# The first expert gather reads unsplit fp32 tokens for four experts, and the hi/lo split moves behind it

## The chip, the cores and the metric

One core of a Trainium2 chip runs a two-layer decoder trunk on 256 tokens of width 1024. The metric is the device time of one execution in microseconds. Numbers are fp32; where the kernel needs accuracy on TensorE at full rate, an operand is split into two fp32r parts (`h`, the rounded value, and `l`, what is left).

## The reference, cut to what matters

```python
def moe(x, router_w, router_b, w_gate, w_up, w_down):
    aff = sigmoid(xt @ router_w); sel_score = aff + router_b
    # best of 4 groups by its two best scores, then the two best experts in it
    ...
    wts = top_aff / sum(top_aff)
    for e in range(N_EXPERTS):                      # 16 experts of width 512
        he = silu(xt @ w_gate[e]) * (xt @ w_up[e])
        y = y + combine[:, e:e + 1] * (he @ w_down[e])

def reference(x, ...):
    for l in range(DEPTH):                          # 2 layers
        y = mixer(x, ...)                           # three attention branches, gated
        x = layer_norm(DN_ALPHA * x + y, ln1_g[l], ln1_b[l])
        y = moe(x, ...)
        x = layer_norm(DN_ALPHA * x + y, ln2_g[l], ln2_b[l])
```

## The kernel before

Each layer is a mixer and then `moe`. In `moe` the 256 tokens (two tiles `t` of 128) are normalised with the statistics `sc` (mean, `rstd`) that the mixer leaves, `aff` and `sel` give the router's scores, and `msk` marks each token's two experts. Each expert has room for 32 tokens of either tile. A count on TensorE (`pm<-msk,cst`) gives each chosen token its place, `onehot` writes it as ones into `Sx`, and `gather` multiplies the tokens with `Sx`: the result `xe` (feature by expert and place) has the 1024 features as 8 blocks `k`. Before the change the tokens for it are split into `x1h` and `x1l`, stored by blocks `k`, and gathered for 8 experts at a time: `gather(0)` in two halves of four `k` (ahead of the first weight products, and behind the first half of `g` of pair 0), `gather(1)` behind `u` of pair 3. The gather results pass through ScalarE and VectorE, which apply the layer norm's gain and shift.

The experts go by pairs `p` = 0 to 7: `g` (gate), `he` by tanh, `u` (up), and one pair later `turn` (transposition of `he`) and `d` (down). Each of `g`, `u`, `d` of a pair is four loads of 1 MiB, named `w_{g|u|d}_{q}_{a}` in the traces (`q` half of the contraction, `a` expert of the pair). They are issued in one fixed order (g0 u0 g1 u1 d0 g2 u2 d1 ...) on SyncE's queue, which is in order: a load whose slot is not yet free holds back all behind it. Slots are 1 MiB tiles of one pool of 25, `big`, taken in turn as they were released; `x1h`, `x1l`, `xe`, `yt`, `acc` come from it too, `target["o"]` reserves slots for these, and `pump` issues as many loads as `held` permits.

At pair 1, `slot_maps(0)` transposes `Sx` into `st` and sums the combine weights (`cs`), and `accumulator(0)` starts the sum `acc` with the token, times ALPHA, times the norm's gain row (`ps`, made by `ln_rows` from `gcol`). VectorE forms it; GpSimd first adds `x1h` and `x1l` up again.

`warm(n)` issues n transposes on TensorE whose results nobody reads. In the traces all engine instructions stand under line 163 (a helper that records them) and all loads under 221, so names of tiles tell them apart. L1196 is the branch of `over`, which treats tokens that did not fit.

## Time and profile before

| | us |
|---|---|
| median of 3 runs | 843.89 (843.61 to 846.78) |
| the profiled execution | 846.54 |
| its span | 844.7 |
| mean granted TensorE clock in it | 0.993 |
| TensorE busy | 815.4 |

The profiled execution is one of the longer ones; times within it are counted from the span's start. The expert stage of the first layer lies at about 203 to 418 us, that of the second at about 620 to 833.

### The profile page before, as it was taken

Reading aid. Unit: us, or ns where it says so; the run is one execution under the profiler, and the core shown is the slowest. Engines: PE = TensorE matmul, PEld = TensorE weight load, DVE = VectorE, ACT = ScalarE, POOL = GpSimd, SP = SyncE. Lnnn points to the kernel's source line nnn. Section 1 sums busy time; section 2 is a strip of 40 time slices with the busy share of each in tenths; the row PEclk is TensorE's granted clock in tenths of the full one; section 3 lists DMA queues with packets and bytes.
Section 4 is the critical chain, followed back from the end, with each engine's and each line's share of the span. In section 5 each row is a group of like instructions: output and inputs, shape, how many; then the busy total and the mean of one; then the engine's idle time right before and its main releaser. Section 6 shows DMA issues by size and latency. Waiting matters only on the chain.

```text
span 844.7 us, 11443 instructions
## 1 busy us (share of the span) xinstructions
PE 815.4 (97%) x4413; PEld 507.3 (60%) x4413; DVE 432.5 (51%) x898; ACT 289.8 (34%) x507; POOL 98.0 (12%) x90
## 2 busy tenths in 40 slices
PE   7999999999999999997999999999999999999986
PEld 7888778889543443333488877788884434333333
DVE  5798565785332232223388976548761412322244
ACT  5445667344111221110355466654331112111112
POOL 0222221002030000000131232110030300000001
PEclk9999999999999999999999999999999999999998
DMA  9993336995599999999898424478948999999992
GB/s 314 336 385 132 123 127 205 393 350 199 216 421 419 419 419 419 419 419 419 323 386 298 163 77 151 150 258 345 357 177 313 419 420 419 419 419 420 418 411 84
DMA packets 65115, 265.24 MB, mean 314 GB/s; under 512 B 6880, under 2 KB 11168, under 8 KB 40992
## 3 DMA queue, kind: packets, MB, share of 16 engines
q1 hardware_dynamic: 64912, 264.39, 80.3%
q8 instruction: 36, 0.59, 0.3%
q14 instruction: 23, 0.19, 0.1%
q10 hardware_dynamic: 144, 0.07, 0.0%
HBM read 263.39 MB, written 1.05 MB: 313 GB/s over the span
## 4 chain that ended last, share of the span: by engine, by line
PE 42%; DMA 7%; DVE 3%; ACT 0%; POOL 0%; issue 0%; POOLq 0%; ACTq 0%; SPq 0%
PE pm L163 36%; DMA w_d<-in_moe_w_down_dram 5%; PE pt L163 3%; PE ps L163 3%; DMA w_u<-in_moe_w_up_dram 2%; DVE bm L163 1%; DVE acc L163 1%; DVE hl L163 0%; POOLq L1406 0%; POOL acc L163 0%; DVE sel L163 0%; ACT hl L163 0%; DVE mv L163 0%; DVE x1l L163 0%; ACT acc L163 0%
## 5 line engine op out<-in xcount | busy, mean ns | idle before, releaser
L163 PE MATMUL pm<-hl,xh 128*128 128x512 f32 (+2 forms) x704 | 227.2, 390 | 1.5 <-ACT hl L163 1.3
L163 PEld LDWEIGHTS pm<-hl,xh 128*128 128x128 f32 x704 | 131.9, 190 | 29.1 <-issue 4.2
L163 DVE TENSOR_TENSOR hl<-w_in,hl 128x1024 fp32r<-128x1024 f32 (+2 forms) x86 | 104.7, 1228 | 60.6 <-ACT hl L163 57.9
L163 PE MATMUL pm<-hl,xl 128*128 128x512 f32 (+2 forms) x352 | 134.0, 381 | 0.3 <-DVE xl L163 0.3
L163 PE MATMUL pm<-w_d,he 128*64 128x512 f32 x512 | 121.0, 604 | 4.2 <-DVEq L1196 2.8
L163 PE MATMUL pm<-w_g,xe 128*64 128x512 f32 x512 | 115.3, 594 | 3.4 <-DVEq L1196 1.7
L163 PE MATMUL pm<-w_u,xe 128*64 128x512 f32 x512 | 114.9, 593 | 1.5 <-DMA w_u<-in_moe_w_up_dram 1.5
L163 ACT CAST hl<-w_in 128x1024 fp32r<-128x1024 f32 (+2 forms) x88 | 85.7, 1001 | 5.7 <-DMA w_in<-in_w_in_dram 4.9
L163 PEld LDWEIGHTS pm<-w_g,xe 128*64 128x64 f32 x512 | 36.9, 137 | 76.6 <-issue 71.8
L163 PEld LDWEIGHTS pm<-w_u,xe 128*64 128x64 f32 x512 | 38.7, 137 | 73.3 <-issue 67.6
L163 PEld LDWEIGHTS pm<-w_d,he 128*64 128x64 f32 x512 | 37.3, 138 | 74.0 <-issue 67.8
L163 PEld LDWEIGHTS pm<-hl,xl 128*128 128x128 f32 x352 | 67.1, 191 | 10.1 <-DVE xl L163 0.5
L163 DVE SCALAR_TENSOR_TENSOR he<-he,pm 128x512 f32<-128x512 f32 x16 | 17.0, 1063 | 87.8 <-ACT he L163 78.9
L163 DVE TENSOR_TENSOR he<-he,pm 128x512 f32<-128x512 f32 x16 | 17.1, 1069 | 67.1 <-PE pm L163 67.1
L163 PE MATMUL pm<-hl,mh 128*128 128x256 f32 (+1 forms) x192 | 46.5, 325 | 0.0
L163 ACT COPY he<-pm 128x512 f32<-128x512 f32 x14 | 8.2, 587 | 109.7 <-PE pm L163 109.7
L163 ACT ACTIVATE he<-pm 128x512 f32<-128x512 f32 x16 | 17.3, 1080 | 80.8 <-PE pm L163 80.8
L163 DVE SCALAR_TENSOR_TENSOR yt<-pm,cs,yt 128x512 fp32r<-128x512 f32 x32 | 22.9, 747 | 43.0 <-ACT yt L163 42.1
L163 ACT ACTIVATE yt<-pm,cs 128x512 fp32r<-128x512 f32 x32 | 20.8, 686 | 67.4 <-PE pm L163 63.2
L163 POOL TENSOR_TENSOR un<-un,su 128x512 f32<-128x512 f32 x24 | 30.7, 1284 | 95.2 <-DVE su L163 56.9
L163 PE MATMUL pm<-hl,oh 128*128 128x512 f32 x128 | 41.3, 394 | 0.0
L163 POOL TENSOR_TENSOR rstd<-rs,cst 128x1 f32<-128x1 f32 (+1 forms) x6 | 4.2, 692 | 309.5 <-DVE rs L163 309.5
(198 smaller groups left out, 1039.6 us busy)
## 6 DMA issues: line engine op xcount, KB each, us to landing
w_g<-in_moe_w_gate_dram SPq DMA_DIRECT2D x64, 1024.0 KB, 13.6
w_u<-in_moe_w_up_dram SPq DMA_DIRECT2D x64, 1024.0 KB, 14.3
w_d<-in_moe_w_down_dram SPq DMA_DIRECT2D x60, 1024.0 KB, 19.0
w_in<-in_w_in_dram SPq DMA_DIRECT2D x36, 1024.0 KB, 13.4
w_br<-in_w_branch_dram SPq DMA_DIRECT2D x8, 1024.0 KB, 5.1
w_wo<-in_w_o_dram SPq DMA_DIRECT2D x8, 1024.0 KB, 5.0
w_d<-in_moe_w_down_dram SPq DMA_DIRECT2D x8, 512.0 KB, 17.1
w_in<-in_w_in_dram SPq DMA_DIRECT2D x4, 768.0 KB, 8.0
```

The costliest lines, as they stand in the source:

```text
L163: r = f(*args, **kw)
```

## The change

- The normalised token is written once, unsplit, in fp32, by ScalarE into `zk`, laid out by the blocks `k`. `gather(0)` takes only experts 0 to 3, by fp32 products of `zk` with `Sx`. Three rounds of gathering take the place of two: 4, 4 and 8 experts.
- Behind the second half of `gather(0)`, `onehot` for experts 4 to 7 and the split of `zk` into `x1h` and `x1l` (`apart1`) follow; `gather(1)` with them comes behind `g` of pair 1, `gather(2)` where `gather(1)` was.
- `accumulator(0)` reads `zk` (strided) instead of GpSimd's sum, and `zk` is given back there.
- At pair 1 `turn(0)` comes ahead of `slot_maps(0)`.
- The mixer's last stage goes tile by tile instead of by halves of the row; fillers fall from 38 to 32; the reserved slots change.

```diff
-WARM = [38, 6, 12]
+WARM = [32, 6, 12]
...
                 piece(0, 0)
+                piece(1, 0)
+                stat(0, 0)
+                logits(0, 1, 0, halves[0])
                 piece(0, 1)
-                stat(0, 0)
-                piece(1, 0)
-                stat(0, 1)
-                logits(0, 1, 0, halves[0])
-                piece(1, 1)
-                logits(1, 1, 0, halves[0])
-                logits(0, 1, 0, halves[1])
                 stat(1, 0)
                 sc = ln_scales(st[:1])
+                logits(0, 1, 0, halves[1])
+                piece(1, 1)
                 logits(0, 1, 1, halves[0])
+                logits(0, 1, 1, halves[1])
+                stat(0, 1)
+                logits(1, 1, 0, halves[0])
...
     def moe(l, sc, lg, rsum):
-        target["o"] = 5
+        target["o"] = 2
         pump()
-        xh = slot([128, T, KD, 128], F32R, "x1h")
-        xl = slot([128, T, KD, 128], F32R, "x1l")
         warm(WARM[0])
-        xv, hv, lv = xt[0].rearrange("p t (q k) -> p t q k", k=KD), xh.rearrange("p t k q -> p t q k"), \
-            xl.rearrange("p t k q -> p t q k")
+        zk = slot([128, T, KD, 128], F32, "zk")
+        xv, zv = xt[0].rearrange("p t (q k) -> p t q k", k=KD), zk.rearrange("p t k q -> p t q k")
         halves = [slice(0, 512), slice(512, 1024)]
-        def normed(t, k):
-            z = xv[:, t, :, k:k + 4]
-            if t == 0:
-                V.tensor_scalar(z, z, sc[0][0], sc[0][1], op0=OP.subtract, op1=OP.mult)
-            else:
-                A.activation(z, z, AF.Identity, bias=sh, scale=sc[1][1])
-        def high(t, k):
-            A.copy(hv[:, t, :, k:k + 4], xv[:, t, :, k:k + 4])
-        def low(E, t, k):
-            E.tensor_tensor(lv[:, t, :, k:k + 4], xv[:, t, :, k:k + 4], hv[:, t, :, k:k + 4].bitcast(F32), op=OP.subtract)
         aff, sel = small(32, "aff"), small(64, "sel")
         z = [aff[:, NE * t:NE * t + NE] for t in range(T)]
-        normed(0, 0)
-        high(0, 0)
-        low(G, 0, 0)
+        def normed(t, k):
+            A.activation(zv[:, t, :, k:k + 4], xv[:, t, :, k:k + 4], AF.Identity, bias=shs[t], scale=sc[t][1])
+        shs = [ln_shift(*z, name=f"sh{t}") for t, z in enumerate(sc)]
         for t in range(T):
             V.scalar_tensor_tensor(z[t], rsum[:, 0:NE], sc[t][0], lg[t][:, 0:NE], op0=OP.mult, op1=OP.subtract)
+        normed(0, 0)
         for t in range(T):
             V.scalar_tensor_tensor(z[t], z[t], sc[t][1], rsum[:, NE:2 * NE], op0=OP.mult, op1=OP.subtract)
         A.activation(aff, aff, AF.Exp)
-        sh = ln_shift(*sc[1])
         normed(1, 0)
         normed(0, 4)
-        high(0, 4)
-        high(1, 0)
         normed(1, 4)
-        high(1, 4)
-        low(G, 0, 4)
+        drop()
+        xt[0] = None
...
-        low(V, 1, 0)
         comb = small(32, "comb")
         ssum = small(2, "ssum")
         c3 = comb.rearrange("p (t e) -> p t e", t=T)
         warm(WARM[1])
         Sx = {}
-        def onehot(r):
-            Sx[r] = work((128, 8, T, CAP), F32R, name="Sx")
+        def onehot(r, es=range(8)):
+            if r not in Sx:
+                Sx[r] = work((128, 8, T, CAP), F32R, name="Sx")
             for t in range(T):
-                z = (pos if r else pc)[:, NE * t + 8 * r:NE * t + 8 * r + 8, None].to_broadcast([128, 8, CAP])
-                V.tensor_tensor(Sx[r][:, :, t], cc("iota")[:, None, :].to_broadcast([128, 8, CAP]), z, op=OP.is_equal)
-        onehot(0)
+                c = NE * t + 8 * r + es[0]
+                z = (pos if (r, es[0]) != (0, 0) else pc)[:, c:c + len(es), None].to_broadcast([128, len(es), CAP])
+                V.tensor_tensor(Sx[r][:, es[0]:es[-1] + 1, t], cc("iota")[:, None, :].to_broadcast([128, len(es), CAP]), z,
+                                op=OP.is_equal)
+        onehot(0, range(4))
         pos = small(32, "pos")
-        low(G, 1, 4)
         V.tensor_tensor(comb, aff, msk, op=OP.mult)
-        drop()
-        xt[0] = None
         target["o"] = 4
-        pump()
+        ROUNDS = [(0, 4), (4, 4), (8, 8)]
         xe = {}
+        x1 = {}
         def gather(r, ks=range(KD)):
+            e0, n = ROUNDS[r]
             if r not in xe:
-                z = [slot([128, 4, 8, T, CAP], F32, "xe") for i in range(2)]
-                xe[r] = [z[k // 4][:, k % 4] for k in range(KD)]
+                z = [slot([128, 32 // n, n, T, CAP], F32, "xe") for i in range(n // 4)]
+                xe[r] = [z[k * n // 32][:, k % (32 // n)] for k in range(KD)]
             for k in ks:
                 o = (ptp if k % 2 == 0 else psc)()
-                ov_ = o.rearrange("p (e t s) -> p e t s", t=T, e=8)
+                ov_ = o[:, :n * T * CAP].rearrange("p (e t s) -> p e t s", t=T, e=n)
                 for t in range(T):
-                    PE.matmul(ov_[:, :, t], xh[:, t, k], Sx[r][:, :, t], start=True, stop=False)
-                    PE.matmul(ov_[:, :, t], xl[:, t, k], Sx[r][:, :, t], start=False, stop=True)
+                    m = Sx[e0 // 8][:, e0 % 8:e0 % 8 + n, t]
+                    if r == 0:
+                        PE.matmul(ov_[:, :, t], zk[:, t, k], m.bitcast(F32), start=True, stop=True)
+                    else:
+                        PE.matmul(ov_[:, :, t], x1[0][:, t, k], m, start=True, stop=False)
+                        PE.matmul(ov_[:, :, t], x1[1][:, t, k], m, start=False, stop=True)
                 g, b = (gpk[:, l, z, k:k + 1] for z in range(2))
                 if k % 2 == 0:
                     A.activation(xe[r][k], ov_, AF.Identity, bias=b, scale=g)
                 else:
                     V.tensor_scalar(xe[r][k], ov_, g, b, op0=OP.mult, op1=OP.add)
+        def apart1():
+            for i, nm in enumerate(("x1h", "x1l")):
+                x1[i] = slot([128, T, KD, 128], F32R, nm)
+            for t in range(T):
+                split(x1[0][:, t], x1[1][:, t], zk[:, t])
...
-                for t in range(T):
-                    h, lo_ = (z[:, t].rearrange("p k q -> p q k").bitcast(F32) for z in (xh, xl))
-                    G.tensor_tensor(xt[0][:, t].rearrange("p (q k) -> p q k", k=KD), h, lo_, op=OP.add)
             for h in range(2):
                 r = ln_rows(z, l, h, psc)
                 for t in range(T):
                     a = xt[0][:, t, halves[h]]
                     if z == 0:
-                        V.scalar_tensor_tensor(a, a, ALPHA, r, op0=OP.mult, op1=OP.mult)
+                        a, b, c = (y.rearrange("p (q k) -> p q k", k=KD) if y is not None else zv[:, t, 64 * h:64 * h + 64]
+                                   for y in (a, None, r))
+                        V.scalar_tensor_tensor(a, b, ALPHA, c, op0=OP.mult, op1=OP.mult)
...
                 if (nm, p, q) == ("g", 0, 0):
                     gather(0, range(4, KD))
+                    onehot(0, range(4, 8))
+                    apart1()
...
             if p == 1:
+                gather(1)
+                turn(0)
...
                 accumulator(0)
+                drop()
...
-            if p % 4 == 3:
-                drop(2)
+            if p in (1, 3, 7):
+                drop(1 + p // 4)
             if p == 3:
-                gather(1)
+                gather(2)
```

The three places below are of VectorE, TensorE and SyncE.

VectorE in the second layer's router chain, from the maximum over the groups to the one-hot matrix: before,

```order
L163 TENSOR_REDUCE gmax<-pr 128x2
L163 MATCH_REPLACE gr<-gmax,gsum 128x8 x2
L163 SCALAR_TENSOR_TENSOR best<-gr,sel 128x32
L163 MAX mx_5366<-best 128x8 x2
L163 MATCH_REPLACE msk<-mx_5366,best 128x16 x2
L163 TENSOR_SCALAR msk<-msk 128x32
L163 TENSOR_TENSOR x1l<-acc,x1h 128x128x4
L163 TENSOR_TENSOR Sx<-cst,pm 128x8x32 x2
L163 TENSOR_TENSOR comb<-aff,msk 128x32
```

and now:

```order
L163 TENSOR_REDUCE gmax<-pr 128x2
L163 MATCH_REPLACE gr<-gmax,gsum 128x8 x2
L163 SCALAR_TENSOR_TENSOR best<-gr,sel 128x32
L163 MAX mx_5386<-best 128x8 x2
L163 MATCH_REPLACE msk<-mx_5386,best 128x16 x2
L163 TENSOR_SCALAR msk<-msk 128x32
L163 TENSOR_TENSOR Sx<-cst,pm 128x4x32 x2
L163 TENSOR_TENSOR comb<-aff,msk 128x32
L163 TENSOR_SCALAR xe<-ps,gpk 128x256 x2
```

The difference `x1l` between the mask and `Sx` is gone, and `Sx` is made for 4 experts (128x4x32) instead of 8.

TensorE in the first layer, from the end of `g` of pair 1 (`w_g` products) to the first product of `u` (`w_u`): before,

```order
L163 MATMUL pm<-w_g_1_0_1694,xe 64x512
L163 MATMUL pm<-w_g_1_1_1714,xe 64x512
L163 MATMUL pt<-cst,Sx 128x128 x4
L163 MATMUL pt<-comb,Sx 128x32 x4
L163 MATMUL pm<-cst,he 128x128 x4
L163 MATMUL ps<-cst,gcol 128x128 x8
L163 MATMUL pm<-w_u_0_0_1716,xe 64x512
```

and now (the last four of the 32 products of `gather(1)` stand ahead):

```order
L163 MATMUL ps<-Sx,x1h 128x4x32
L163 MATMUL ps<-Sx,x1l 128x4x32
L163 MATMUL ps<-Sx,x1h 128x4x32
L163 MATMUL ps<-Sx,x1l 128x4x32
L163 MATMUL pm<-cst,he 128x128 x4
L163 MATMUL pt<-cst,Sx 128x128 x4
L163 MATMUL pt<-comb,Sx 128x32 x4
L163 MATMUL ps<-cst,gcol 128x128 x8
L163 MATMUL pm<-w_u_0_0_1716,xe 64x512
```

The gather's second round has come in behind `g`, and the turn of `he` (`pm<-cst,he`) stands ahead of the transposes of `Sx` and of the sums with `comb`.

SyncE in the first layer, the last of the loads of `u` of pair 2, the four of `d` of pair 1, and the first two of `g` of pair 3, with the semaphores that each waits for (DMAHW is a DMA lane; the number behind a tile's name is a running one): before,

```order
L221 DMA w_u_1_1_2192<-in_moe_w_up_dram 128x2048 [waits DMAHW3_49,PE_49]
L221 DMA w_d_0_0_2194<-in_moe_w_down_dram 128x2048 [waits DMAHW4_49,PE_49]
L221 DMA w_d_0_1_2215<-in_moe_w_down_dram 128x2048 [waits DMAHW5_49,PE_49]
L221 DMA w_d_1_0_2217<-in_moe_w_down_dram 128x2048 [waits DMAHW6_49,PE_49]
L221 DMA w_d_1_1_2270<-in_moe_w_down_dram 128x2048 [waits DMAHW7_49,PE_49]
L221 DMA w_g_0_0_2272<-in_moe_w_gate_dram 128x2048 [waits DMAHW0_49,PE_49]
L221 DMA w_g_0_1_2282<-in_moe_w_gate_dram 128x2048 [waits DMAHW1_49,PE_49]
```

and now:

```order
L221 DMA w_u_1_1_2181<-in_moe_w_up_dram 128x2048 [waits DMAHW3_49,PE_49]
L221 DMA w_d_0_0_2183<-in_moe_w_down_dram 128x2048 [waits DMAHW4_49,PE_49]
L221 DMA w_d_0_1_2193<-in_moe_w_down_dram 128x2048 [waits DMAHW5_49,PE_49]
L221 DMA w_d_1_0_2195<-in_moe_w_down_dram 128x2048 [waits DMAHW6_49,PE_49]
L221 DMA w_d_1_1_2295<-in_moe_w_down_dram 128x2048 [waits DMAHW7_49,DVE_49,Activation_49]
L221 DMA w_g_0_0_2297<-in_moe_w_gate_dram 128x2048 [waits DMAHW0_49,PE_49]
L221 DMA w_g_0_1_2307<-in_moe_w_gate_dram 128x2048 [waits DMAHW1_49,PE_49]
```

The load `w_d_1_1` waited for TensorE and now waits for VectorE and ScalarE: the slot that it takes was that of a gate weight of pair 1 and is now that of `zk`. The second layer's rows have the same change.

## Rows read from the trace of the kernel before

**Rows 1.** Part 1 of the page: busy time of the engine, share of the span and instructions.

```profile
PE 815.4 (97%) x4413; PEld 507.3 (60%) x4413; DVE 432.5 (51%) x898; ACT 289.8 (34%) x507; POOL 98.0 (12%) x90
```

**Rows 2.** The windows view: for each stretch its length, then busy us and instructions of each engine, the granted TensorE clock, the DMA share and GB/s.

```profile
212.00:216.00 4.00, 3.98 (x18) 3.59 (x20) 2.17 (x4) 1.55 (x2) 0.96 (x1) 0.59 0.49 145
228.00:400.00 172.00, 166.78 (x862) 63.95 (x860) 50.22 (x77) 23.37 (x32) 7.53 (x2) 1.00 1.01 420
399.60:403.00 3.40, 3.40 (x11) 1.20 (x9) 0.00 (x0) 0.00 (x0) 0.00 (x0) 0.50 1.01 410
760.00:820.00 60.00, 57.45 (x294) 21.75 (x290) 19.82 (x27) 9.14 (x13) 0.00 (x0) 1.00 1.01 418
```

**Rows 3.** The chain that ended last, from 755 to 830 us: start us, us, what.

```profile
781.41 19.89 DMA w_u<-in_moe_w_up_dram
...
801.37 19.92 DMA w_d<-in_moe_w_down_dram
```

**Rows 4.** The timeline of TensorE at the end of the first layer's experts: start us, us, engine, line, operation, out<-in, shapes, count, and in brackets the idle time before it and its releaser.

```profile
376.03 3.65 PE L163 MATMUL pm<-w_g,xe 128*64 128x512 f32 x16 [0.35 <-DMA w_g<-in_moe_w_gate_dram]
381.02 3.65 PE L163 MATMUL pm<-w_g,xe 128*64 128x512 f32 x14 [1.34 <-DMA w_g<-in_moe_w_gate_dram]
...
391.00 3.65 PE L163 MATMUL pm<-w_u,xe 128*64 128x512 f32 x14 [0.76 <-DMA w_u<-in_moe_w_up_dram]
...
398.56 5.35 PE L163 MATMUL pm<-w_d,he 128*64 128x512 f32 x16 [2.77 <-DVEq L1196]
```

**Rows 5.** The waits of TensorE from 610 to 835 us: engine, line, what was waited for, us in total, times, longest.

```profile
PE pm L163 <- DMA w_d<-in_moe_w_down_dram: 1.3, 1, 1.3
PE pm L163 <- DMA w_u<-in_moe_w_up_dram: 0.8, 1, 0.8
```

**Rows 6.** The timeline of TensorE, columns as in rows 4, around the first half of the gather: in the first layer (three rows) and in the second.

```profile
210.63 0.41 PE L163 MATMUL pm<-msk,cst 128*128 128x32 f32 x2 [1.60 <-DVE msk L163]
...
212.02 0.55 PE L163 MATMUL pt<-Sx,x1h 128*128 128x256 f32 x1 [0.29 <-DVE Sx L163]
...
215.53 0.65 PE L163 MATMUL pm<-w_g,xe 128*64 128x512 f32 x2
...
628.75 0.36 PE L163 MATMUL pt<-Sx,x1h 128*128 128x256 f32 x1 [0.28 <-DVE Sx L163]
...
630.92 3.65 PE L163 MATMUL pm<-w_g,xe 128*64 128x512 f32 x16
```

**Rows 7.** The timeline of all engines, columns as in rows 4, along the router's chain of the second layer.

```profile
621.24 0.55 DVE L163 TENSOR_SCALAR acc<-acc,mv,rstd 128x512 f32<-128x512 f32 x1
...
621.39 0.80 POOL L163 TENSOR_TENSOR rstd<-rs,cst 128x1 f32<-128x1 f32 x1 [0.26 <-DVE rs L163]
621.43 4.34 PE L163 MATMUL pt<-cst 128*128 128x128 f32 x38
...
623.07 3.34 POOL L163 TENSOR_TENSOR x1l<-acc,x1h 128x512 fp32r<-128x512 f32 x2 [0.88 <-ACT aff L163]
...
623.66 1.09 DVE L163 TENSOR_TENSOR sel<-aff,rb 128x64 f32<-128x64 f32 x1
624.78 0.23 DVE L163 TENSOR_TENSOR pr<-sel 128x64 f32<-128x64 f32 x1
...
625.82 0.64 DVE L163 SCALAR_TENSOR_TENSOR best<-gr,sel 128x32 f32<-128x32 f32 x1
...
627.23 1.06 DVE L163 TENSOR_TENSOR x1l<-acc,x1h 128x512 fp32r<-128x512 f32 x1
...
627.37 0.41 PE L163 MATMUL pm<-msk,cst 128*128 128x32 f32 x2 [1.60 <-DVE msk L163]
...
627.62 0.85 PE L163 MATMUL pt<-cst 128*128 128x128 f32 x6
628.19 0.75 DVE L163 TENSOR_TENSOR Sx<-cst,pm 128x256 fp32r<-128x256 f32 x2
```

**Rows 8.** The same view where pair 1's `g` ends and its `he` and the accumulator are formed (second layer).

```profile
646.98 7.04 PE L163 MATMUL pm<-w_g,xe 128*64 128x512 f32 x32
...
654.15 7.54 POOL L163 TENSOR_TENSOR acc<-x1h,x1l 128x1024 f32<-128x1024 f32 x2 [24.45 <-PE pm L163]
...
656.41 1.10 ACT L163 ACTIVATE he<-pm 128x512 f32<-128x512 f32 x1
...
656.70 7.09 PE L163 MATMUL pm<-w_u,xe 128*64 128x512 f32 x32
...
657.55 1.07 DVE L163 SCALAR_TENSOR_TENSOR he<-he,pm 128x512 f32<-128x512 f32 x1 [1.42 <-ACT he L163]
...
658.53 0.68 DVE L163 SCALAR_TENSOR_TENSOR acc<-acc,ps 128x512 f32<-128x512 f32 x1
...
661.72 1.88 DVE L163 SCALAR_TENSOR_TENSOR acc<-acc,ps 128x512 f32<-128x512 f32 x3 [2.51 <-POOL acc L163]
```

**Rows 9.** The view of one tile on SyncE's queue: first the issue (duration in ns, first and last start), then the time from issue to landing; a `w_g` load issued at 619.2 us into an empty queue, and the last down weight of pair 1 (`w_d_1_1`) at 654.1.

```profile
L221 SPq DMA_DIRECT2D w_g<-in_moe_w_gate_dram x1: 327/327/327, 619.2 to 619.2; - x1
...
DMA to landing us min/median/max: 5.0/5.0/5.0
...
L221 SPq DMA_DIRECT2D w_d<-in_moe_w_down_dram x1: 328/328/328, 654.1 to 654.1; - x1
...
DMA to landing us min/median/max: 12.2/12.2/12.2
```

More of the change, by code (lines that the diff above doesn't have):

```diff
@@ L397, in ln_rows, with ln_shift @@
         return p
-    def ln_shift(mean, rstd):
-        sh = small(1, "sh")
+    def ln_shift(mean, rstd, name="sh"):
+        sh = small(1, name)
         V.scalar_tensor_tensor(sh, mean, -1.0, rstd, op0=OP.mult, op1=OP.mult)
@@ L855, in mixer @@
                 piece(0, 0)
+                piece(1, 0)
+                stat(0, 0)
+                logits(0, 1, 0, halves[0])
                 piece(0, 1)
-                stat(0, 0)
-                piece(1, 0)
-                stat(0, 1)
-                logits(0, 1, 0, halves[0])
-                piece(1, 1)
-                logits(1, 1, 0, halves[0])
-                logits(0, 1, 0, halves[1])
                 stat(1, 0)
                 sc = ln_scales(st[:1])
+                logits(0, 1, 0, halves[1])
+                piece(1, 1)
                 logits(0, 1, 1, halves[0])
+                logits(0, 1, 1, halves[1])
+                stat(0, 1)
+                logits(1, 1, 0, halves[0])
+                stat(1, 1)
+                sc += ln_scales(st[1:])
                 logits(1, 1, 0, halves[1])
                 logits(1, 1, 1, halves[0])
-                logits(0, 1, 1, halves[1])
                 logits(1, 1, 1, halves[1])
-                stat(1, 1)
-                sc += ln_scales(st[1:])
                 drop(3)
@@ L1179, in product @@
             def product(k, a, w):
-                x_ = xe[p // 4][k][:, 2 * (p % 4) + a].rearrange("p t s -> p (t s)")
+                r = min(p // 2, 2)
+                x_ = xe[r][k][:, 2 * p + a - ROUNDS[r][0]].rearrange("p t s -> p (t s)")
                 PE.matmul(o[64 * a:64 * a + 64], x_, w, start=(k == 0), stop=(k == KD - 1))
@@ L1211, in over @@
                     for k in range(KD):
-                        for j, z in enumerate((xh, xl)):
+                        for j, z in enumerate((x1[0], x1[1])):
                             for t in range(T):
@@ L1314, in moe @@
                 tc.mark_branch_hint_location(f"over{l}", engines=[mybir.EngineType.PE])
-            if p == 1:
+            if p == 2:
                 target["o"] = 6
-            if p == 2:
-                target["o"] = 7
             if p == 3:
@@ L1328, in moe @@
             up_("g", p, pg)
+            if p == 0:
+                target["o"] = 6
             if p == 1:
+                gather(1)
+                turn(0)
                 slot_maps(0)
-                turn(0)
             he = hts[p] = work(name="he")
```

## The prediction, on record before the run

> **What bounds the kernel now.** I read the page first: TensorE is busy 97% of the span [rows 1]. The windows view adds the other half: from 228 to 400 us (experts of the first layer) and from 760 to 820 (of the second) the DMA share is 1.01 at about 420 GB/s, while TensorE is busy 166.78 us of 172 and 57.45 of 60 [rows 2]. Which of the two sets the end is told by the chain of waits: its last pieces but the closing ones are two 19.9 us runs of `w_d` and `w_u` loads, not matmuls [rows 3]. A pair of experts is 12 loads of 1 MiB, 30 us at 420 GB/s, and its matmuls take less, so the loads held when the stage starts are eaten up and the last pairs wait for their weights: 0.35 + 1.34 + 0.76 = 2.45 us in the first layer [rows 4] and 0.8 + 1.3 = 2.1 in the second [rows 5]. So each expert stage ends when the weight stream ends. An edit there counts by two things: when the stream begins, and whether it is ever interrupted. TensorE's own work has only these 2.45 and 2.1 us of room before it is the bound.
>
> The profiled execution took 846.54 us, 2.65 over the median of 843.89. Two stretches at half clock make that up. The granted clock is 0.59 from 212 to 216 and 0.50 from 399.6 to 403 [rows 2]. From its first product to the first of `w_g`, the first half of the first layer's gather took 215.53 - 212.02 = 3.51 us, the same work in the second layer 630.92 - 628.75 = 2.17 [rows 6]: 1.34 lost. The sixteen `w_d` products at 398.56 took 5.35 against 3.65 for sixteen others [rows 4]: 1.70 lost. 846.54 - 3.04 = 843.5. Both stretches come behind idle time of TensorE, 1.60 us [rows 6] and 2.77 [rows 4]; but the 1.60 us of the second layer [rows 7] were followed by none. I sum differences on the second layer's rows, which have no such stretch, and set them against the median.
>
> **The change, part by part.** All times are of the second layer before; the first layer does the same.
>
> *Router chain.* `normed` on VectorE, the first rounded copies and GpSimd's differences `x1l` go. `sel` (128x64) took 1.09 us and ended with GpSimd's first difference; `pr` of the same size right behind took 0.23. `best` took 0.64 and ended with GpSimd's second, where the larger `pr` took 0.23 [rows 7]. Without GpSimd I take 0.85 and 0.4 off. Two one-column `sh` steps come ahead, but the 0.55 us `normed` goes, and GpSimd's second `rstd`, 0.80 beside it, may get shorter [rows 7]: together between 0 and -0.3. The mask comes 1.25 to 1.55 us earlier. Behind it VectorE's `x1l` of 1.06 goes and `Sx` is halved; but TensorE's count and its 6 filler products still run 1.1 us from the mask (627.37 to 628.47 [rows 7]), so the gather, which began 1.38 behind it, at 628.75 [rows 6], wins only 0.25 more. The first gather itself costs as before: half the experts, but an fp32 product is issued in two parts, so 16 issues again ahead of the first `w_g` product. That one comes **1.7 us** earlier; bounds 1.3 (no `rstd` gain, `best` barely shorter) and 1.9. The first layer's half-clock stretch may go too (-1.34 on a disturbed execution, nothing on the median): the idle time ahead of the mask's product shrinks from 1.6 to about 1.0, since the mask comes 1.25 earlier and the fillers fall from 38 to 32, 0.7 us at 4.34 / 38 = 0.114 each [rows 7].
>
> *Mixer's last stage.* The same pieces in another order; the last `rs` comes out where it was, as the last piece still ends the product stream. 0, bounds -0.4 and +0.4.
>
> *Second gather.* 32 products of 128 columns are added behind `g` of pair 1, on TensorE, in the path of everything there. None of this form is in the trace. Below: 32 x 0.068 = 2.2 us, if one takes half of a 256-column product (2.17 / 16 = 0.136 [rows 6]). Above: the 128-column fillers, 0.114 each [rows 7], so 3.65 us. These are the nearest in columns, and hardly faster than 256 columns: I take **3.65**. TensorE ends each layer's stage 3.65 - 1.7 = 1.95 later, less than its waits of 2.45 and 2.1, so by itself this is hidden.
>
> *Conversions.* The `x1` copies and differences go to pair 0, where VectorE and ScalarE have room (29 to 33% and 14 to 15% busy over the stage [rows 2]): 0. GpSimd's sum for `acc`, 7.54 us, goes; VectorE waited 2.51 for it [rows 8], and behind it stood only the second step of pair 1's `he`, which needs `u`, ready at 663.8, anyway: 0.
>
> *The load queue.* This decides. Three loads go to slots that are free at the mixer's end, earlier than before, but into a queue idle anyway: 0. One goes later, the last of pair 1's down weights, `w_d_1_1` (the last fences of the change): SyncE's queue is in order, and this load now waits for VectorE's last read of `zk`, the fourth `acc` of pair 1, where it waited for the end of `g`. Before: issued at 654.1, right behind the last `w_g` product (646.98 + 7.04 [rows 8]), it landed 12.2 later, at 666.3, because others were ahead of it; a load issued into an empty queue landed in 5.0 [rows 9]. The stream is thus 7.2 us ahead at this point, and a hold up to that length is free.
>
> Now, without the 1.7: `g` ends at 654.0, the gather at 657.6. Turn, maps and `gcol` rows run there as before, to the first `w_u` at 656.70 + 3.65 = 660.35 [rows 8]. On ScalarE the copy of `he`, the cast of `st` and then tanh (1.10) come in order behind the turn; tanh, which ended at 657.5, ends 2.8 later, at 660.3 (less than 3.65 since the turn now stands ahead of the maps). VectorE's `he` follows, 1.07, to 661.4; then four `acc`. They took 0.68 and 1.88 / 3 = 0.63 [rows 8] on contiguous rows. Now one input is `zk`, read at steps of 512 bytes. `he`, the same operation at the same step, took 1.07 [rows 8]; bounds 0.63 and 1.07, and I take 1.0, being nearest in kind to `he`. The last ends at 665.4, the load is issued at 665.5 and lands at 670.5: 4.2 later than before. The hold is 11.4, the cover 7.2. The eight loads ahead run dry, and everything behind is late by 4.2 - 1.7 = **2.5 us per layer**, 5.0 in both; TensorE's own shift of 1.95 lies inside it. With contiguous prices: 663.9, 2.7 - 1.7 = 1.0 per layer.
>
> The Trainium skill has a rule that speaks to this price (SBUF — State Buffer, in the section Door 1: The DMA port swizzle, its note on cachelines): consecutive accesses within one 16-byte line run at full bandwidth, each access to a new line pays a penalty. By that rule the `acc` with `zk` is slower than the contiguous one and the sum is the 5.0, without it the 2.0; the rows of `he` and `acc`, 1.07 against 0.63 to 0.68, agree, but for a strided output, not a strided input.
>
> **Sum.** 2 x 2.5 = +5.0 on 843.9: **848.9 us** (851.5 for an execution with both half-clock stretches).
>
> **Rivals.**
> - *Hold covered, TensorE the bound.* If the last `acc` ends before 661.2, as it would if tanh and `he` were done during the second gather, or the loads ahead took longer, the stream is not interrupted. It would then win 1.7, but TensorE's 1.95 uses up the waits: 1.95 - 2.45 = -0.5 and 1.95 - 2.1 = -0.15. Together -0.65: 843.2. For it: tanh needs only `g`. Against: on ScalarE it stands behind the turn's copy, in program order. 0.17.
> - *Short hold.* The strided input costs nothing and the 128-column products half: hold shorter by 1.5 + 1.45, 2.5 - 2.95 = -0.45 per layer: 843.0. One of the two alone gives +2.0 or +2.1, 845.9 to 846.0. For it: the output is contiguous. Against: the row of the fillers. 0.25 for either or both.
> - *More than the hold.* The empty queue makes later loads late too, or TensorE, idle longer before its last `w_d`, falls to half clock where it hadn't (1.34 to 1.7 each): +6.5 to +9, 850.5 to 853. For it: such stretches follow waits of 1.6 to 2.8 us in this trace, and the waits grow. 0.13.
> - *All gains, no cost.* Cheap products and a covered hold: -1.7 on each stream and TensorE far enough ahead, with the mixer's order winning 0.4 per layer: -4.2, 839.7. 0.08.
> - Forecast: 0.37, from 846.3 (0.25 less `acc` each, more lead) to 850.
>
> **Numbers.** This measurement tells a difference of about 0.5%, 4.2 us, from none. Slower than 848.1: most of the forecast's case (0.31 of 0.37) and the third rival (0.13), 0.44. Faster than 839.7: 0.08. The rest, 0.48, is between. The range from 842.4, somewhat under the short hold, to 852.5, inside the third rival, leaves out about 0.1 on either side; the forecast's own is 846.3 to 851.
>
> **What will show it.** Right: `w_d_1_1` issued some 11 us behind the end of `g` of pair 1, landing after 5 us, with a gap in the DMA rate near 660 to 666; `acc<-zk` about 1.0 each; `sel` near 0.23; 3.65 us of `Sx` products ahead of the turn; TensorE's waits for pair 7's weights longer by 0.5 per layer. Wrong: no gap in the rate (first rival), `acc` at 0.65 or gather products of 0.07 (second), new half-clock stretches (third). The weakest step is the 5.0 us landing in an empty queue against a stream that I take to have nothing else in it.

## The result, and the profile after

The changed kernel takes 854.62 us (median of 4 runs, 850.37 to 855.46), the kernel before 845.34 beside it; the ratio is 1.011, with a 95% interval of 1.0087 to 1.0133. The profiled execution took 854.18, with a span of 852.4, against 846.54 and 844.7. Its first part of the page:

```profile
PE 819.5 (96%) x4465; PEld 510.8 (60%) x4465; DVE 435.1 (51%) x910; ACT 295.1 (35%) x515; POOL 71.4 (8%) x80
```

TensorE is busy 4.1 us more than in [rows 1], and the span is 7.7 us longer: about half of what the profiled execution lost is waiting.

I read the new trace in the order of the prediction's steps. The router's chain of the second layer, from the timeline of all engines (columns as in rows 4):

```profile
625.51 0.15 DVE L163 TENSOR_SCALAR rs<-mv 128x1 f32<-128x1 f32 x1
...
628.34 0.22 DVE L163 TENSOR_TENSOR sel<-aff,rb 128x64 f32<-128x64 f32 x1
...
629.64 0.20 DVE L163 SCALAR_TENSOR_TENSOR best<-gr,sel 128x32 f32<-128x32 f32 x1
...
630.74 0.41 PE L163 MATMUL pm<-msk,cst 128*128 128x32 f32 x2 [0.32 <-DVE msk L163]
...
633.57 0.65 PE L163 MATMUL pm<-w_g,xe 128*64 128x512 f32 x2
```

`sel` takes 0.22 and `best` 0.20, against 1.09 and 0.64 in [rows 7]; the wait ahead of the mask's product is 0.32 instead of 1.60. From the second `rs` to the first `w_g` product it is 633.57 - 625.51 = 8.06 us.

Pair 1, from the same view:

```profile
656.46 0.33 PE L163 MATMUL pt<-Sx,x1h 128*128 128x128 f32 x1
...
659.97 0.28 PE L163 MATMUL ps<-Sx,x1l 128*128 128x128 f32 x1
660.08 0.63 PE L163 MATMUL pm<-cst,he 128*128 128x128 f32 x4
...
662.79 7.09 PE L163 MATMUL pm<-w_u,xe 128*64 128x512 f32 x32
662.81 1.06 DVE L163 SCALAR_TENSOR_TENSOR he<-he,pm 128x512 f32<-128x512 f32 x1
...
663.78 3.93 DVE L163 SCALAR_TENSOR_TENSOR acc<-zk,ps 128x512 f32<-128x512 f32 x4
```

The second gather lasts from 656.46 to the turn (`pm<-cst,he`) at 660.08, 3.6 us; `u` starts at 662.79; `he` takes 1.06 and the four `acc<-zk` 3.93, 0.98 each. They end at 667.7. On SyncE's queue, the four loads of `d` of pair 1 and the next four (start, us from the first to the last issue), and the view of the fourth alone:

```profile
650.11 18.00 SPq L221 DMA_DIRECT2D w_d<-in_moe_w_down_dram  x4
668.19 2.53 SPq L221 DMA_DIRECT2D w_g<-in_moe_w_gate_dram  x4
```

```profile
L221 SPq DMA_DIRECT2D w_d<-in_moe_w_down_dram x1: 328/328/328, 667.8 to 667.8; - x1
...
DMA to landing us min/median/max: 5.2/5.2/5.2
```

The fourth is issued at 667.8, right behind the last `acc`, and lands 5.2 us later. The DMA engines meanwhile, in the windows view (columns as in rows 2):

```profile
664.00:668.00 4.00, 4.00 (x21) 1.30 (x19) 3.71 (x4) 0.00 (x0) 0.00 (x0) 1.00 0.10 39
668.00:672.00 4.00, 4.00 (x22) 1.43 (x20) 1.71 (x3) 0.00 (x0) 0.00 (x0) 1.00 0.78 266
```

In the kernel before, the same two stretches:

```profile
664.00:668.00 4.00, 4.00 (x24) 1.71 (x21) 1.58 (x3) 0.16 (x1) 0.00 (x0) 1.00 1.01 418
668.00:672.00 4.00, 4.00 (x23) 1.64 (x22) 2.48 (x4) 0.42 (x1) 0.00 (x0) 1.00 1.01 418
```

39 and 266 GB/s, where the kernel before moves 418 here and 418 to 420 over the experts [rows 2]. The missing bytes, (420 - 39) x 4 + (420 - 266) x 4 = 2140 GB/s x us, are 5.1 us of the stream. (The gaps of all kernels below are worked out in this way, from the windows of 4 us between 660 and 676.)

The chain that ended last has the same last load as before [rows 3]:

```profile
809.13 19.91 DMA w_d<-in_moe_w_down_dram
```

The last `w_d` load now ends at 829.04 instead of 821.29, 7.75 later. This is not all from the gaps. At the end of the first layer's experts, the timeline of TensorE:

```profile
392.54 3.65 PE L163 MATMUL pm<-w_u,xe 128*64 128x512 f32 x14 [0.76 <-DMA w_u<-in_moe_w_up_dram]
...
403.07 5.15 PE L163 MATMUL pm<-w_d,he 128*64 128x512 f32 x16 [5.74 <-PEq L1195]
```

The last weights of pair 7's `u` come 1.54 us later than in [rows 4] (392.54 against 391.00). But the `w_d` products behind them start 4.51 later (403.07 against 398.56): the wait ahead of them is 5.74 instead of 2.77, and it is no longer VectorE's sequencer (DVEq) but TensorE's own (PEq) that ends it, at the branch of `over`. The view of that line lists the branches of TensorE, shortest, median and longest in ns, in the kernel after and in the one before:

```profile
L1195 PEldq COMPARE_BRANCH  x2: 350/3142/5935, 396.7 to 794.9; - x2
```

```profile
L1196 PEldq COMPARE_BRANCH  x2: 398/448/499, 395.2 to 787.1; - x2
```

The first layer's branch, at 396.7, took 5.94 us, where it took 0.40 before (the shorter of the two there). In the 6 us from 397 to 403 the DMA view counts one transfer (packets, MB, share) on the queue for instructions, of 0.02 MB:

```profile
q8 instruction: 1, 0.02, 1.1%
```

### The profile page after: what moved, and what is told of

It reads as the page before. It is cut to its first block, busy times and chain, and to the rows that moved or that the text cites. A ratio compares the mean times of both kernels' runs of the same rounds, so it can differ in the third digit from the quotient of the medians.

```text
span 852.4 us, 11546 instructions
## 1 busy us (share of the span) xinstructions
PE 819.5 (96%) x4465; PEld 510.8 (60%) x4465; DVE 435.1 (51%) x910; ACT 295.1 (35%) x515; POOL 71.4 (8%) x80
## 4 chain that ended last, share of the span: by engine, by line
PE 42%; DMA 7%; DVE 2%; issue 1%; ACT 0%; POOL 0%; POOLq 0%; SPq 0%; ACTq 0%
PE pm L163 35%; DMA w_d<-in_moe_w_down_dram 5%; PE pt L163 4%; PE ps L163 3%; DMA w_u<-in_moe_w_up_dram 2%; DVE acc L163 0%; DVE bm L163 0%; DVE hl L163 0%; ACT hl L163 0%; POOL hl L163 0%; POOLq L1407 0%; POOL acc L163 0%; DVE aff L163 0%; ACT acc L163 0%; ACT wt L163 0%
## 5 line engine op out<-in xcount | busy, mean ns | idle before, releaser
L163 PE MATMUL pm<-w_u,xe 128*64 128x512 f32 x512 | 116.9, 594 | 1.7 <-DMA w_u<-in_moe_w_up_dram 1.5
L163 POOL TENSOR_TENSOR wt<-wt 128x256 f32<-128x256 f32 (+1 forms) x36 | 27.4, 774 | 108.7 <-DVE wt L163 107.7
```

The costliest lines, as they stand in the source:

```text
L163: r = f(*args, **kw)
```

## The experiments

Three theories stood against each other. **The hold**: the tile `zk` keeps a load back and the stream pauses. **TensorE**: the 3.65 us of the second gather are what costs. **The branch**: code is read late. Beside the experiments stand 13 to 17 runs of the kernel before on the same chip, with medians of 843.52 to 844.14; the ratios are to those.

### The mark of the branch earlier

```diff
-            if p == 6:
+            if p == 5:
                 tc.mark_branch_hint_location(f"over{l}", ...)
```

> The changed kernel with one edit: the mark that announces the branch of `over` on TensorE stands at pair 5 instead of pair 6. Theory of the branch: in the changed kernel TensorE's own compare-and-branch of the first layer took 5.94 us (0.40 to 0.50 before) and held the first `w_d` products of pair 6 back by 5.74, where VectorE's branch alone would have held them 2.77; announced earlier it takes under 1 us, the wait is about 2.8 again on VectorE, and the median falls by about 3, to 851 to 852. Rival, that it is a matter of chance or of the weight stream: branch and median unchanged, 854 to 855.

852.88 us (850.82 to 856.63), ratio to before 1.0108. The branch, in the same view:

```profile
L1195 PEldq COMPARE_BRANCH  x2: 350/3220/6090, 395.8 to 795.0; - x2
```

The branch is as long as without the edit. The instructions that the marks make stand at the same places in both kernels (at 0.8 us, and right behind the first layer's branch), so the edit moved nothing, and no theory was tested by it.

### The accumulator at pair 0

```diff
-            if p == 1:
-                accumulator(0)
-                drop()
             up_("u", p, pu)
             V.tensor_tensor(hv, hv, uv_, op=OP.mult)
+            if p == 0:
+                accumulator(0)
+                drop()
```

> The changed kernel with the accumulator formed at pair 0, behind `u`, and `zk` given back there, so that its slot is free before a load asks for it. Theory of the hold (a gap of 4.9 us in the weight stream per layer, because one load waits for the last reader of `zk`): the DMA rate has no zero between 240 and 250 and between 664 and 670 us; the stream ends 4.9 earlier in each layer, but TensorE's waits for the last weights are only 2.25 and 3.5, so that much is won: 854.6 - 5.7 = 848.9, the branch's 3 us still in it. Rival, TensorE's added 3.65 us per layer are what costs: the gap goes and the time stays, 853 to 855.

847.59 us (842.03 to 849.17), ratio 1.0037 (1.0017 to 1.0057): 7.0 us less than the changed kernel, 6 by the two ratios. The windows:

```profile
660.00:664.00 4.00, 4.00 (x20) 1.42 (x21) 1.69 (x5) 1.02 (x2) 0.00 (x0) 1.00 0.95 399
664.00:668.00 4.00, 4.00 (x22) 1.41 (x20) 0.73 (x1) 0.00 (x0) 0.00 (x0) 1.00 0.81 272
```

399 and 272 GB/s: the gap is (84 + 592) / 420 = 1.6 us instead of 5.1. The hold is the larger part of the loss; the 1.6 that stay are not explained by it. In the profiled execution the first layer's branch still takes 5.93 us.

### The accumulator's steps twice

```diff
+                        for _ in range(2):
                             V.scalar_tensor_tensor(a, b, ALPHA, c, ...)
```

> The changed kernel with each of the four steps that form `acc` from `zk` done twice, which changes no value: 3.9 us more of VectorE work ahead of the release of `zk`, in each layer. Theory of the hold: the gap in the stream grows from 4.9 to 8.8 us and the time by 2 x 3.9 = 7.8, to 862.4. Rival, TensorE is the bound: VectorE has room there, time unchanged within 1 us, 854 to 855.5.

854.02 us (853.33 to 855.42), ratio 1.0118: no change, a miss. The windows:

```profile
664.00:668.00 4.00, 4.00 (x22) 1.58 (x22) 3.79 (x7) 0.53 (x1) 0.00 (x0) 1.00 0.53 219
668.00:672.00 4.00, 4.00 (x22) 1.40 (x20) 3.93 (x5) 0.00 (x0) 0.00 (x0) 1.00 0.69 225
672.00:676.00 4.00, 4.00 (x25) 1.76 (x22) 3.42 (x5) 0.31 (x1) 0.00 (x0) 1.00 1.01 360
```

The gap is (804 + 780 + 240) / 420 = 4.3 us, less than 5.1. The reason is in SyncE's order, where the pool, which hands out slots in the order in which it reckons them free, has given `zk`'s slot to a load two places further on:

```order
L221 DMA w_d_1_1_2299<-in_moe_w_down_dram 128x2048 [waits DMAHW7_49,PE_49]
L221 DMA w_g_0_0_2301<-in_moe_w_gate_dram 128x2048 [waits DMAHW0_49,PE_49]
L221 DMA w_g_0_1_2311<-in_moe_w_gate_dram 128x2048 [waits DMAHW1_49,DVE_49,Activation_49]
```

`w_d_1_1` now waits for TensorE: it is issued at 668.2, when the first half of pair 1's `u` (begun at 664.5) is through, and that costs nearly the same. The load two places on then waits 4.8 us for `acc`. So it is not `zk`'s reader as such: one slot is missing at pair 1, and what comes free next is late too. How much of that is the slot and how much the 3.65 us on TensorE, the kernels with a held tile below tell.

### 32 products on TensorE alone, in the kernel before

```diff
             if p == 1:
+                warm(32)
                 slot_maps(0)
                 turn(0)
```

> The kernel before with 32 products whose result nobody reads added on TensorE behind `g` of pair 1, 3.65 us per layer, at the place of the second gather; nothing else moves. If TensorE's waits for the last weights (2.45 and 2.1 us) are its room: 2 x 3.65 - 4.55 = +2.75, 846.5 to 848.5. If TensorE is the bound throughout: +7.3, about 852. If the room is larger than I read: 0.

848.18 us (846.92 to 849.76), ratio 1.0058 (1.0038 to 1.0078); the profiled execution took 846.92. The windows:

```profile
660.00:664.00 4.00, 4.00 (x22) 1.32 (x20) 3.44 (x5) 0.45 (x1) 1.12 (x1) 1.00 0.93 387
664.00:668.00 4.00, 4.00 (x22) 1.41 (x20) 1.21 (x2) 0.00 (x0) 0.00 (x0) 1.00 0.95 342
```

A gap of (132 + 312) / 420 = 1.1 us per layer. The time alone would fit the first expectation (846.5 to 848.5); the gap says why that reading falls short: TensorE's waits for weights are not free room for added work, since the queue waits for slots that TensorE frees. The loads of `g` behind `d` of pair 1 begin at 663.30 instead of 660.37. The branch takes 2.02 us here and hides behind VectorE's. The median stands 4.7 over the kernel before; two gaps of 1.1 give 2.2 of it. The profiled execution is the shortest of the four, so what the longer ones lost was not seen.

### 48 more instructions ahead of everything, changed kernel

```diff
     G.memset(best, FAR)
+    zz = cpool.tile([128, 32], F32, name="zz")
+    nc.gpsimd.memset(zz, 0.0)
+    pz = ptp("pz")
+    for i in range(12):
+        nc.tensor.matmul(pz[0:32, 0:1], zz, zz[:, 0:1], start=True, stop=True)
```

> The changed kernel with 48 more instructions on TensorE (12 one-column products of a zero tile) in the first 4 us, where TensorE waits for its first data, so that all its later code lies 48 instructions further on; nothing else moves. Theory of the code's place: in the changed kernel the first layer's branch stood at TensorE's instruction 4295 and waited 5.94 us, during which a 16 KiB block of code was read, in the kernel before it stood at 4244 and took 0.40, with 64 instructions more than that 2.02. A place 48 further is past the edge at which the next block is asked for: branch under 1 us, TensorE's wait ahead of pair 6's `w_d` about 2.8 on VectorE, median 850 to 851.5. Rival, the branch is slow because the queues are fuller in the changed kernel, whatever the place: 854 to 855.

849.99 us (849.73 to 850.34), ratio 1.0069. The branches, and the first products of `w_d` behind the one of the first layer:

```profile
L1200 PEldq COMPARE_BRANCH  x2: 353/418/482, 395.4 to 791.2; - x2
```

```profile
398.75 6.56 PE L163 MATMUL pm<-w_d,he 128*64 128x512 f32 x16 [2.76 <-DVEq L1200]
```

0.48 at most, and the wait is 2.76, VectorE's again. From 395.4 to 398.1 us nothing moves on the queue for instructions; one such transfer comes ahead of the branch, from 388 to 395.4:

```profile
q8 instruction: 1, 0.02, 0.9%
```

The median is 4.6 us lower by work that does nothing, 3.5 by the two ratios, since the two kernels did not run side by side, and 3.8 between the two profiled executions (854.18 and 850.34). 3.0 of it is the wait. The runs now agree within 0.6 us, where those of the changed kernel spread over 5.

### 52 more instructions, kernel before

The same edit with `range(13)` in the kernel before.

> The kernel before with 52 instructions added at the same place in the first 4 us, which puts the first layer's branch at instruction 4296, where the changed kernel has it. Theory of the code's place: its branch now takes about 5.9 us and TensorE waits for it instead of for VectorE: +3 to +4.7 (a longer half-clock stretch behind), 846.5 to 848. Rival, the place does not matter: 843.5, as without them.

848.45 us (846.69 to 849.56), ratio 1.0056 (1.0039 to 1.0073).

```profile
L1201 PEldq COMPARE_BRANCH  x2: 353/3020/5687, 392.1 to 787.4; - x2
```

```profile
398.22 6.40 PE L163 MATMUL pm<-w_d,he 128*64 128x512 f32 x16 [5.69 <-PEq L1201]
```

The stall of 5.69 us, made to order in the kernel before, +4.4 us in the median. The last two runs together show the cause: the place of the branch in TensorE's code, nothing else of the change. 2.9 of the 4.4 are the longer wait; the rest is not accounted for. It cannot be put down to the half clock behind a longer wait: sixteen `w_d` products took 6.40 here and 5.15 in the changed kernel behind the long wait, 5.35 [rows 4] and 6.56 (the last kernel) behind the short one.

### The accumulator at pair 0 and the 48 instructions

> The accumulator formed at pair 0 (which gave 847.6) and the 48 instructions at the start, both. If the hold and the branch are two separate costs, 847.6 - 3 to 4 = 843.6 to 844.6, level with the kernel before. If the branch's wait was cover for something else, such as the loads: 846 to 847.6.

843.95 us (843.37 to 845.72), ratio 1.0000 (0.9990 to 1.0009). The two costs are separate and add, as near as these medians tell (the 48 instructions are worth 3.6 here): with both gone, the change is worth nothing either way. Its profiled execution still has the gap of 1.6 us (256 and 412 GB/s from 660 to 668).

### A slot fewer in the kernel before, alone and with the products

```diff
             if p == 1:
+                dz = slot([128, T, D], F32, "dz")
+                nc.gpsimd.memset(dz[:, 0, 0:1], 0.0)
+                warm(32)                    # second kernel only
                 slot_maps(0)
                 turn(0)
...
             if p == 1:
                 accumulator(0)
+                nc.vector.tensor_copy(small(1, "dzr"), dz[:, 0, 0:1])
+                drop()
```

> The kernel before with one tile of the pool taken behind `g` of pair 1 and given back behind the accumulator, with nothing in it: a slot fewer for the loads over that time, as the changed kernel has, and no work on TensorE. `w_d_1_1` then waits for the first half of `u` of pair 1, 660.4 instead of 654.1, 6.3 us later. The gaps measured so far (4.9 for a hold of 11.1) say that 6.2 us of hold are free: no gap or under 0.5 us, time as before, 843.5 to 845. If a slot fewer is by itself the changed kernel's loss: a gap of 4 to 5 per layer, 851 to 853.

> The same tile held in the kernel before, and the 32 products on TensorE behind `g` of pair 1. Alone the products cost a gap of 1.0 per layer, alone the tile is expected to cost 0 to 0.5. If the two act on one another, since the slot that `w_d_1_1` gets instead is freed by TensorE, which is 3.65 later: hold 9.9, gap 3.7 to 4.3 per layer, +7.4 to +8.6, 851 to 852.5. If the costs only add: 1.0 to 1.5 per layer, 848 to 849 (the branch as with the products alone).

The tile alone: 846.10 us (843.91 to 849.73), ratio 1.0021 (1.0004 to 1.0038), somewhat over the 843.5 to 845 expected. Tile and products: 857.57 (853.77 to 860.12), ratio 1.0170; its profiled execution took 853.77. The windows, the first kernel's one row and the second's two:

```profile
660.00:664.00 4.00, 4.00 (x22) 1.35 (x20) 1.95 (x4) 0.00 (x0) 1.98 (x1) 1.00 0.98 379
```

```profile
664.00:668.00 4.00, 4.00 (x20) 1.31 (x20) 3.32 (x5) 0.65 (x1) 1.32 (x1) 1.00 0.39 160
668.00:672.00 4.00, 4.00 (x20) 1.29 (x18) 1.20 (x4) 0.00 (x0) 0.00 (x0) 1.00 0.87 303
```

The tile alone leaves a gap of 164 / 420 = 0.4 us, the products alone 1.1, both 3.6. They act on one another: SyncE waits for TensorE at that load, which is issued at 660.7 with the tile alone, when the first half of pair 1's `u` is through, and TensorE is 3.65 us later with the products. That is a pause of the changed kernel's kind (3.6 us of its 5.1), rebuilt in the kernel before. The median went 5 us over the upper end that I expected; no trace of the longer executions was taken, so that part stays open.

### Eight experts by fp32 products

```diff
-        ROUNDS = [(0, 4), (4, 4), (8, 8)]
+        ROUNDS = [(0, 8), (8, 8)]
...
-                gather(1)                   # pair 1
                 turn(0)
```

with the accumulator at pair 0 and one slot more reserved from the start to pair 2.

> The changed kernel with the first gather taking eight experts by fp32 products of `zk`, so that the round of four at pair 1 is gone, and the accumulator at pair 0: the router's gain without the 3.65 us on TensorE and without the extra tile held over pair 1. If the two costs found (a slot short at pair 1, and TensorE's 3.65 us) are all there is besides the branch, the stream starts 1.5 to 1.8 earlier in either layer and is not interrupted: 843.5 - 3.2 = 840.3, if the branch (at instruction 4232 or so) does not stall. If fp32 products of 256 columns cost twice the split ones, the gather's first half lasts 2 us longer and nothing is won: 843.5 to 845.

853.34 us (852.23 to 854.14), ratio 1.0106, a miss. TensorE's first gather, and the DMA engines from 220 to 228 us, in this kernel and in the changed one:

```profile
210.32 1.10 PE L163 MATMUL pt<-Sx,zk 128*128 128x256 f32 x4
...
212.12 1.03 PE L163 MATMUL pt<-Sx,zk 128*128 128x256 f32 x4
```

```profile
220.00:224.00 4.00, 4.00 (x20) 1.82 (x20) 3.09 (x4) 2.66 (x3) 0.00 (x0) 1.00 0.02 4
224.00:228.00 4.00, 4.00 (x20) 1.29 (x18) 1.60 (x2) 1.08 (x1) 0.00 (x0) 1.00 0.51 158
```

```profile
220.00:224.00 4.00, 4.00 (x22) 1.32 (x20) 2.53 (x3) 1.09 (x2) 0.00 (x0) 1.00 0.37 86
224.00:228.00 4.00, 4.00 (x22) 1.41 (x20) 0.00 (x0) 0.00 (x0) 0.00 (x0) 1.00 1.00 422
```

Each row is two 256-column fp32 products, issued in two parts; with the row left out between them, eight issues take 212.12 - 210.32 = 1.80 us, 0.22 each, where the split ones took 2.17 / 16 = 0.136 [rows 6] and the 128-column fp32 ones of the changed kernel 0.11 (four in 0.45 us). So fp32 at 256 columns costs twice its 128-column price. And the stream starts later: two loads instead of three are issued before it begins, and from 204 to 228 us the windows add up to 5.9 us missing against the changed kernel, (154 + 123 + 82 + 264) x 4 / 420. I take the cause to be that `zk` beside two `xe` and both `x1` takes a slot from these loads; that was not tried by itself.

### The second gather in the middle of `d` of pair 0

```diff
-                gather(1)
                 turn(0)
                 slot_maps(0)
...
                 def between():
+                    if p == 1:
+                        gather(1)
                     turn(p)
```

on top of the accumulator at pair 0 and the 48 instructions.

> The accumulator at pair 0, the 48 instructions at the start, and the second gather 11 us later, in the middle of `d` of pair 0, where the loads are far ahead. If its place behind `g` of pair 1 caused the last gap (1.4 us), the stream is not interrupted and is 1.8 earlier per layer, and TensorE, 1.8 later, becomes the bound: 842.5 to 843.5. If its 3.65 us cost the same wherever they stand: 844, as with the gather behind `g`.

841.39 us (839.11 to 842.00), ratio 0.9959 (0.9941 to 0.9977): faster than both kernels. The windows:

```profile
660.00:664.00 4.00, 4.00 (x27) 2.23 (x23) 1.27 (x4) 0.62 (x2) 0.00 (x0) 1.00 1.01 424
664.00:668.00 4.00, 4.00 (x36) 3.54 (x36) 2.60 (x6) 2.21 (x4) 0.00 (x0) 1.00 1.02 424
```

No gap. The one difference to the kernel with 843.95 us is the place of the gather, so its place behind `g` of pair 1 caused the last gap. The same products, now 12.2 us behind the end of that `g` (650.13 to 662.34), cost the stream nothing; I take the reason to be that no load waits then for a slot that they delay. The time is 1 us under the lower end that I expected.

### Half of the split early

```diff
         gather(0, range(4))
+        onehot(0, range(4, 8))
+        apart1(1)                           # blocks 4 to 7
...
                 if (nm, p, q) == ("g", 0, 0):
-                    gather(0, range(4, KD))
-                    onehot(0, range(4, 8))
-                    apart1()
+                    gather(3, range(4, KD)) # eight experts, split
...
                     if p == 1:
-                        gather(1)
+                        gather(1, range(4))
+                        apart1(0)           # blocks 0 to 3
+                        drop()
```

on top of the accumulator at pair 0, with 80 idle instructions at the start and one slot more reserved in places.

> From the last one: behind the first half of `g` of pair 0 the tokens' blocks 4 to 7 are already split and gathered for eight experts, so that the second gather has only the blocks 0 to 3 of four experts left, 1.8 us instead of 3.65 (fp32 products of 128 columns); the split of blocks 0 to 3 follows at pair 1. No more tiles are held than in the kernel before. If the stream's start and TensorE's added time are what is left to win: 1.8 us earlier start, TensorE 1.8 - 1.8 = 0 later, 843.7 - 3.6 = 840. If the split does not get done in the 3.65 us ahead of the second half: TensorE waits there 1 to 2 us, 842 to 844.

841.72 us (840.62 to 843.38), ratio 0.9971 (0.9959 to 0.9982): no better than the last. TensorE around the second half of the gather:

```profile
212.05 3.65 PE L163 MATMUL pm<-w_g,xe 128*64 128x512 f32 x16
215.63 0.75 PE L163 MATMUL pt<-Sx,x 128*128 128x256 f32 x4
```

The split is done in time (no wait at 215.63), and TensorE's 1.8 us are saved, but they go into longer waits: in the first layer's experts TensorE waits 2.0 us for weights (1.3 and 0.7), where it waited 0.5 in the kernel above, and 1.6 instead of 1.3 in the second's.

## Why the prediction was wrong

**The sign and the mechanism of the hold were right; a cost was left out, and a term was too small**: 848.9 with a range to 852.5 was forecast, 854.6 came, and the range held the time only without the branch (849.99 with the 48 instructions).

*Router chain: right.* 1.7 us forecast. Before, VectorE's step right behind the last `rs` began at 621.24 [rows 7] and `w_g` at 630.92 [rows 6], 9.7 us; after, `rs` began at 625.51 and `w_g` at 633.57, 8.06 us, or 7.9 from its end of 0.15: 1.8 won. `sel`, `best` and the fillers came out as worked out, and so did 0 for the mixer's order (the first layer's last `rs` starts at 204.28, before at 204.42). At 212 us the clock is at 1.00, so that half-clock stretch is not in this profile.

*Second gather: its price right, its effect not.* 3.6 us. I had set it against TensorE's waits for the last weights and called it hidden by itself. The 32 products alone cost a gap of 1.1 us per layer, since the loads' slots are freed by TensorE; the first rival rested on the same reading and falls with it. In the sum this cost does not stand beside the hold: the 3.6 us are part of the hold's length.

*The hold: right in its place and length.* Forecast: `acc` 1.0 each, the load 11.4 us later than before behind the end of `g`. Measured: 0.98, and 667.8 against 656.5, the end of `g`, 11.3. The landing, 5.0 forecast, took 5.2. The rule of the Trainium skill on 16-byte lines (SBUF — State Buffer, Door 1: The DMA port swizzle) spoke for the higher price; the trace agrees, 0.98 against 0.63 to 0.68 in [rows 8], now for a strided input alone. (The prediction called `he` a case of a strided output; the kernel has `he` read at that step too.)

*The cover: mis-sized.* I took 7.2 us, the difference of two times from issue to landing, 12.2 and 5.0. Three kernels give it better. The four loads of `d` of pair 1 on SyncE's queue, in the kernel before, with the tile alone, and with tile and products:

```profile
647.60 6.82 SPq L221 DMA_DIRECT2D w_d<-in_moe_w_down_dram  x4
```

```profile
647.91 13.10 SPq L221 DMA_DIRECT2D w_d<-in_moe_w_down_dram  x4
```

```profile
651.23 16.59 SPq L221 DMA_DIRECT2D w_d<-in_moe_w_down_dram  x4
```

Against the 6.82 us of the kernel before, `w_d_1_1` was held 6.3 us with the tile alone and the gap was 0.4, 9.8 with the products too and the gap was 3.6, 11.2 (18.00) in the changed kernel and the gap 5.1. So by my estimate some 5.9 to 6.2 us are free, and what goes beyond is lost nearly whole (1.4 us more hold, 1.5 more gap). The term of the sum was 4.2 and should have been 5.1: 0.9 per layer, 1.8 in all. Why a landing in a full queue overstates the lead (that the following load's bytes are already among those that have come) was not tried.

*The branch: not in the sum at all.* +3.0 us by the wait alone, up to 4.6 by the medians (854.62 to 849.99). [rows 4] showed the branch's wait, 2.77 on VectorE's sequencer, and I took it for a constant. I counted the instructions that the change adds to TensorE for their time, not for their place. The third rival, with 0.13, had a longer half-clock stretch behind a longer wait as a possibility, but no reason for the longer wait; in the profiled execution the products behind it lost nothing more (5.15 against 5.35).

By terms: 5.0 forecast + 1.8 for the cover + 3.0 to 4.6 for the branch = 9.8 to 11.4, against 9.3 measured beside the same runs of before and 10.5 to 11.1 beside those of the experiments. Without the stalled branch the gaps go with the times: twice the gap less the 1.8 us won is +6.8 for the changed kernel with the 48 instructions (a gap of 5.2), -0.4 with the accumulator at pair 0 too, and -3.6 with the gather late; measured +6.0, 0.0 and -2.8.

## What to carry to other kernels

Where loads run ahead through a pool, ask for every added tile and every added piece of work which release the next load waits for: a tile held longer and work added on the engine that frees slots may each cost little and together much more (gaps of 0.4 and 1.1 us alone, 3.6 together); and read what a hold may last from the bytes of the stream, not from issue-to-landing times. An edit that adds instructions ahead of a branch moves it in the code: look at the branch's own duration in the trace before blaming the edit. Added work is cheapest where the queue is not waiting for what that work delays.

## What the runs showed of the hardware

- TensorE's branch of the first layer took 0.39 to 0.40 us with 4232 to 4244 of TensorE's instructions ahead of it in the trace (three kernels), 5.69 to 6.09 with 4295 to 4297 (five), 1.87 to 2.02 with 4306 and 4307 (two), 0.48 with 4344 to 4347 (four), whatever else the kernels changed; the second layer's took 0.35 to 0.90 in all of them. These are the profiled executions, one of each kernel. A transfer on the queue for instructions falls into the 6 us of the long one, and ahead of the branch with the 48 instructions. The Trainium skill (Runtime: NRT & Kernel Launch, Instruction fetch mechanics) says that an engine's code is fetched in 16 KiB blocks, in sequence, and that a taken branch to a block not yet there waits for its transfer. The traces agree in kind: the wait comes and goes with the branch's place, and a transfer of 0.02 MB falls into it.
- An fp32 product (the fillers' transposes aside) stands twice in these traces, as two issues: an issue of 128 columns took 0.11 us, of 256 columns 0.22. An issue of a split fp32r product took 0.11 us at 128 columns (3.6 us for 32) and 0.12 to 0.14 at 256.
- A VectorE step of 128x512 that reads one fp32 input at steps of 512 bytes took 0.98 us, where the contiguous one took 0.63 to 0.68.
